# The output projection as seven products of half blocks instead of eight

## Chip, cores and metric

The kernel runs on one core of one Trainium2 chip. The metric is the device time of one execution in microseconds (us); a run list gives its median over several runs. The engines are named as in the profile: PE (matmul, with its weight loader PEld), DVE (vector), ACT (scalar), POOL (general purpose), and SP, which issues most transfers. Each engine executes its own instructions strictly in the order of the program; an instruction that waits holds up all that stand behind it on that engine.

## Reference

One layer of a hybrid attention backbone: 1024 tokens, 1024 channels, two attention branches, a gated merge, an output projection, a residual with LayerNorm, and a SwiGLU feed-forward with a convolution. The part that the change touches:

```python
def _merge_branches(o_a, o_b, gate_logits, w_branch_a, w_branch_b, w_out):
    g_a, g_b = jnp.split(jax.nn.sigmoid(gate_logits), 2, axis=-1)
    return (g_a * (o_a @ w_branch_a) + g_b * (o_b @ w_branch_b)) @ w_out
...
        h = x * (1.0 + scale1) + shift1
        y = _latent_token_mixer(h, kv_ctx, w_in[l], b_in[l], attn_sink[l], q_norm_g[l], k_norm_g[l],
                                w_branch_a[l], w_branch_b[l], w_out[l], rope)
        x = _layer_norm(DEEPNORM_ALPHA * x + gate1 * y, ln1_g[l], ln1_b[l])

        h = x * (1.0 + scale2) + shift2
        y = _conv_ffn(h, w_up[l], conv_w[l], conv_b[l], w_down[l])
```

## The kernel before

Data lies transposed: channels on the 128 partitions (8 feature tiles f of 128 channels, KT = 8), tokens along the free dimension (T = 1024, two halves of HALF = 512). Every float32 matrix product is done as three matmuls with split operands (`mm3`, lines 90 to 92): each operand is a rounded high part and the low part that is left, and the products high x high, low x high and high x low are added up in PSUM. So each weight and each activation must first be split: a cast for the high part (`split`, line 82 on ACT) and a subtraction for the low part (line 87, on DVE or POOL as the caller says).

The order of stages on PE is: modulation and projections, gates (`gate`, from the weights `wg`, about 100 to 310 us), attention with the branch products A, attention B, the branch products B (tiles `b1_f`, 720 to 763.8 us here), the output projection (tiles `y`, 763.8 to about 857), then the up projection (tiles `u`), the convolution, and the down projection. PE's order in the projection is written out by hand (`manual_schedule`); a scheduler places the other engines' instructions around it, and they then run in that order.

Branch B and the merge. For f = 2 to 7, `b1_f` is multiplied by its gate on DVE (line 1111), and `merge` adds branch A (line 1089) and splits the sum m into `mh` (ACT) and `ml` (DVE).

Output projection. `wout_start` loads one block of `w_out` (128 x 1024, through a raw buffer `rwo`), splits it (`hwo` on ACT, `lwo` on DVE), loads the residual tiles `z` from x and scales them on POOL (line 1083). `y_pair(f, s)` computes the output tiles f and f + 1 for the tokens s: 2 x 8 x 3 matmuls into one PSUM tile of the pool `big` (3 buffers). Then `wout_z` adds gate1 times the result to `z` (line 1222, DVE), and `ln_add` adds up the sum `zs` (POOL for the first half of the tokens, DVE for the second) and the sum of squares `zq` (a square on ACT, an addition on DVE) over the eight tiles. The first half of the tokens is done for all f, then the second half; its last four tiles are done in two slices of 256 tokens (LN1_S is 512, 256 and 256 tokens), so that LayerNorm can begin with a part.

LayerNorm. `ln_steps` makes a list of steps: small matmuls `sta` that add up `zs` and `zq` over the channels (lines 1179, 1180), the variance (DVE, one POOL power, line 1193), a broadcast of mean and scale by PE (line 1201), and for each f an `apply` (lines 1209 to 1213) and `emit1`, which makes the next stage's inputs `B` and the next residual `zo`. `tick` is called between matmuls and releases the next step when enough matmul columns have gone by; LN1_F is the wait before the first step and LN1_D the waits after it, for each of the three slices. A larger number puts a step later in PE's order.

Tiles in SBUF come from a list of slots: `ht` takes one and `hput` gives one back, so that a new tile waits for the last reader of the slot that it gets.

Of the kernel before, what the change touches and what calls it, by code (L numbers as in the profile page):

```python
# [7 lines left out]
F32 = mybir.dt.float32  # L8
# [29 lines left out]
LN1_F = 3500.0, 2000.0, 2000.0  # L38
LN1_D = (2500.0, 2000.0, 2500.0), (2500.0, 1000.0, 700.0), (2500.0, 1000.0, 700.0)
# [30 lines left out]
def layer_kernel(  # L70
# [53 lines left out]
    zd = [dpool.tile([P, T], F32, tag=f"zd{f}", name=f"zd{f}") for f in range(KT)]  # L124
    sgd = [dpool.tile([P, T], F32, tag=f"sg{f}", name=f"sgd{f}") for f in range(2 * KT)]
# [640 lines left out]

    sgp = [None]

    def gate(f, hf):
# [303 lines left out]
    wts = {}  # L1073

    def wout_start(f, rtag="raw"):
        wts[f] = weight(w_out[f], f"wo{f}", 8, tag=None if f < 4 else "wd" if f & 2 else "w", he=nc.scalar,
                        le=nc.vector, rtag=rtag)
        for hf in (0, 1):
            if f < 4:
                zt_[f, hf] = ht(f"z{f}_{hf}", (P, 2, HALF))  # L1080
            z = zv(f, hsl(hf))
            nc.sync.dma_start(z, xT[f][:, hsl(hf)])
            nc.gpsimd.tensor_scalar(out=z, in0=z, scalar1=ALPHA, scalar2=0.0, op0=ALU.mult, op1=ALU.add)

    def merge(f, parts=(slice(0, T),)):
        m = bT[0, f]
        mh, ml = ht(f"mh{f}", dt=R32), ht(f"ml{f}", dt=R32)
        for s in parts:
            nc.vector.tensor_tensor(out=m[:, s], in0=m[:, s], in1=bT[1, f][:, s], op=ALU.add)
            split(m[:, s], mh[:, s], ml[:, s], nc.scalar, nc.vector)  # L1090
        hput(f"bT0_{f}", f"bT1_{f}")
        mrg.append((mh, ml))
# [4 lines left out]
    for f in range(2, KT):  # L1097
# [14 lines left out]
        merge(f, [slice(hs[0] * HALF, (hs[-1] + 1) * HALF) for hs in halves])  # L1112
# [3 lines left out]
        if f in (5, 7):  # L1116
            wout_start(f // 2 - 2, None)
# [103 lines left out]
    def wout_z(f, s, ps, first):  # L1221
        nc.vector.scalar_tensor_tensor(out=zv(f, s), in0=ps, scalar=modc[:, 16 + f:17 + f], in1=zv(f, s),
                                       op0=ALU.mult, op1=ALU.add)
        ln_add(zv(f, s), zs, zq, s, first, f"a{f}_{s.start}", nc.vector,
               nc.vector if s.start else nc.gpsimd)
# [12 lines left out]
    def emit1(f, s):  # L1238
# [8 lines left out]
        if hf:  # L1247
            if f < 4 and c.start == 0:
                tp["v", f] = ht(f"v{f}", (P, 2, HALF))
            v = tp["v", f % 4][:, f // 4, c]  # L1250
            o = z
        else:
            o = ht(f"zo{f}", (P, w))
            hput(f"zo{f}")
            if f % 2:
                nc.gpsimd.tensor_scalar(out=o, in0=z, scalar1=lnx[:, 16 + f:17 + f], scalar2=lnx[:, 24 + f:25 + f],
                                        op0=ALU.mult, op1=ALU.add)
            else:
                residual(o, f, z)
# [60 lines left out]
    def y_pair(f, s, first=False):  # L1320
        w = s.stop - s.start
        ps = big(f"y{f}_{s.start}_{w}")
        for a in (0, 1):
            mm_ticked(ps[:, a * HALF:a * HALF + w], wts[f + a], mrg, s)
        for a in (0, 1):
            wout_z(f + a, s, ps[:, a * HALF:a * HALF + w], first and a == 0)
# [610 lines left out]
```

## Time and profile before

| what | value |
|---|---|
| median of 3 runs | 1523.68 us (1523.13 to 1526.4) |
| profiled execution | 1523.1 us, its span 1521.3 us |
| PE busy | 1503.2 us (99%) |
| DVE, ACT, POOL busy | 1168.3, 786.1 and 751.3 us |
| chain that ended last | PE 92% |
| output projection, tiles `y` | 763.8 to about 857 us |
| its matmuls | 288 of 512 columns, 192 of 256 |

The profile is one execution. The span is from its first to its last instruction, and 1.8 us lie around it. In a row of groups the columns are line, engine, operation, tiles with their shapes, count, busy time and mean duration (ns), and after the second bar the idle time of that engine just before, with what ended it. In a row of the timeline the first number is the start, the second the duration of the group; in brackets stands the idle time before it and the instruction that ended it. In a row of waits stand the total, how often, and the longest. In a row of one tile or line come shortest, median and longest duration in ns, then the first and the last start. A window's row has busy time and count of PE, PEld, DVE, ACT and POOL, the granted clock of PE, the share of time in which DMA engines were busy, and GB/s.

### The profile page before, as it was taken

What the parts mean: (1) busy time and instruction counts of PE and PEld (TensorE: products, weight loads), DVE (VectorE), ACT (ScalarE), POOL (GpSimd) and SP (SyncE); (2) the same over time, 40 slices, a digit from 0 to 9 for tenths busy, and PEclk for the clock granted to TensorE, in tenths of its full rate; (3) what the DMA queues carried; (4) which work ended last, traced back from release to release, by engine and by line L of the source; (5) the groups of instructions that cost most, each with busy time, mean ns of one, the idle gap of its engine ahead of it and who ended that gap; (6) DMA issues with size and microseconds to landing.
All of it is one profiled execution on the core that took longest, in us unless ns stands there. A gap on an engine that the chain in (4) does not pass through costs nothing.

```text
span 1521.3 us, 22183 instructions
## 1 busy us (share of the span) xinstructions
PE 1503.2 (99%) x7812; PEld 1263.3 (83%) x7812; DVE 1168.3 (77%) x1751; ACT 786.1 (52%) x1303; POOL 751.3 (49%) x727
## 2 busy tenths in 40 slices
PE   8999999999999999999999999999999999999997
PEld 7888888888988888887888998888888888888887
DVE  6667986539988787877865788888888888557884
ACT  5322222439988677667234555444444444435552
POOL 0356532426776677766124346666666773111121
PEclk9999999999999999999999999999999999999998
DMA  9777672322234576653541322333344448996731
GB/s 370 266 242 242 223 252 87 106 82 68 67 108 104 131 172 167 153 121 89 207 160 42 104 77 98 111 111 111 111 111 111 112 111 238 340 271 210 255 105 56
DMA packets 114399, 232.09 MB, mean 153 GB/s; under 512 B 13200, under 2 KB 28048, under 8 KB 114192
## 3 DMA queue, kind: packets, MB, share of 16 engines
q1 hardware_dynamic: 99056, 201.82, 39.8%
q0 software_dynamic: 10400, 20.19, 8.8%
q10 hardware_dynamic: 4832, 8.68, 1.5%
q8 instruction: 61, 1.00, 0.3%
q14 instruction: 50, 0.41, 0.1%
HBM read 179.45 MB, written 65.86 MB: 161 GB/s over the span
## 4 chain that ended last, share of the span: by engine, by line
PE 92%; DVE 3%; ACT 2%; issue 1%; DMA 1%; POOL 1%; SPq 0%; DVEq 0%; ACTq 0%; POOLq 0%
PE ptr L604 5%; PE p L90 4%; PE p L91 4%; PE p L92 4%; PE g L90 4%; PE g L92 4%; PE g L91 4%; PE av L627 4%; PE av L628 3%; PE b L90 3%; PE b L92 3%; PE b L91 3%; PE s L496 3%; PE s L497 3%; PE c L90 2%; PE c L92 2%
## 5 line engine op out<-in xcount | busy, mean ns | idle before, releaser
L616 DVE TENSOR_TENSOR ptl<-ptr,pth 128x512 fp32r<-128x512 f32 x195 | 128.2, 685 | 20.2 <-ACT pth L615 18.0
L547 ACT ACTIVATE p<-p,nm 128x1280 f32<-128x1280 f32 (+2 forms) x128 | 139.8, 1093 | 6.6 <-DVE p L545 5.9
L87 DVE TENSOR_TENSOR ld<-rd,hd 128x1024 fp32r<-128x1024 f32 x77 | 94.8, 1250 | 50.5 <-ACT hd L82 48.3
L615 ACT CAST pth<-ptr 128x512 fp32r<-128x512 f32 x195 | 111.3, 590 | 30.3 <-PE ptr L604 28.7
L82 ACT CAST hd<-rd 128x1024 fp32r<-128x1024 f32 x77 | 79.3, 1048 | 82.2 <-PE p L92 55.7
L604 PEld LDWEIGHTS ptr<-identr,pb 128*128 128x128 f32 x944 | 96.3, 140 | 23.7 <-ACT pb L550 3.0
L604 PE MATMUL ptr<-identr,pb 128*128 128x128 f32 x944 | 107.5, 245 | 1.5 <-ACT pb L550 1.0
L87 POOL TENSOR_TENSOR wlg<-wg,whg 128x512 fp32r<-128x512 f32 x32 | 48.6, 1529 | 121.7 <-ACT whg L82 80.8
L627 PE MATMUL av<-pth,VT 128*128 128x512 f32 x236 | 104.2, 441 | 0.5 <-ACT side L639 0.3
L90 PE MATMUL p<-hd 128*128 128x512 f32 x264 | 103.2, 391 | 0.0
L92 PE MATMUL p<-hd,ld 128*128 128x512 f32 x264 | 102.8, 389 | 0.0
L91 PE MATMUL p<-ld,hd 128*128 128x512 f32 x264 | 102.7, 389 | 0.0
L90 PE MATMUL g<-hh,whg 128*128 128x512 f32 x256 | 99.9, 390 | 0.0
L92 PE MATMUL g<-hh,wlg 128*128 128x512 f32 x256 | 99.7, 389 | 0.0
L91 PE MATMUL g<-hl,whg 128*128 128x512 f32 x256 | 99.6, 389 | 0.0
L628 PE MATMUL av<-ptl,VT 128*128 128x512 f32 x236 | 97.5, 413 | 0.3 <-DVE ptl L616 0.2
L545 DVE TENSOR_SCALAR_CACHE_REDUCE p<-s,cvt,nmc 128x1024 f32<-128x1024 f32 x64 | 84.2, 1317 | 5.2 <-PE s L497 5.2
L496 PE MATMUL s<-KL,q 128*128 128x512 f32 (+2 forms) x192 | 73.6, 384 | 1.3 <-DVE p L545 0.8
L497 PE MATMUL s<-KL,q 128*128 128x512 f32 (+2 forms) x192 | 71.8, 374 | 0.0
L783 ACT ACTIVATE sg<-g,bgc 128x512 f32<-128x512 f32 x32 | 22.0, 686 | 96.2 <-PE g L92 91.4
L82 ACT CAST wS<-s 128x512 fp32r<-128x512 f32 x76 | 45.3, 620 | 48.7 <-POOL s L1236 47.9
L82 ACT CAST wA<-ru 128x512 fp32r<-128x512 f32 x57 | 35.5, 623 | 62.6 <-PE d L92 33.6
(434 smaller groups left out, 4866.9 us busy)
## 6 DMA issues: line engine op xcount, KB each, us to landing
wml<-in_wmodT_dram SPq DMA_DIRECT2D x48, 512.0 KB
ru<-in_w_up_dram SPq DMA_DIRECT2D x38, 512.0 KB
rd<-td SPq DMA_DIRECT2D x55, 256.0 KB
rd<-sd SPq DMA_DIRECT2D x44, 256.0 KB
rd<-in_w_dn_dram SPq DMA_DIRECT2D x33, 256.0 KB
wm<-in_wmodT_dram SPq DMA_DIRECT2D x16, 512.0 KB
wg<-in_w_g_dram SPq DMA_DIRECT2D x32, 256.0 KB
sgd<-sg ACTq DMA_DIRECT2D x32, 256.0 KB
```

The lines of the kernel that those rows point to most:

```text
L82: nc.scalar.copy(hi, src)
L87: lo_eng.tensor_tensor(out=lo, in0=src, in1=hi.bitcast(F32), op=ALU.subtract)
L90: nc.tensor.matmul(ps, a[0], b[0], start=start, stop=False, skip_group_check=resumed)
L91: nc.tensor.matmul(ps, a[0], b[1], start=False, stop=False, skip_group_check=resumed)
L92: nc.tensor.matmul(ps, a[1], b[0], start=False, stop=stop, skip_group_check=resumed)
L496: nc.tensor.matmul(o, self.q[0][:, hs], ks, start=True, stop=False)
L497: nc.tensor.matmul(o, self.q[1][:, hs], ks, start=False, stop=stop)
L547: nc.scalar.activation(row, row, AF.Exp, bias=self.nm[:, hs], scale=-1.0, accum_out=self.sm[:, hs])
L604: i = nc.tensor.transpose(tr[:, h * P:(h + 1) * P], self.bits[:, h, n * P:(n + 1) * P], identr)
L616: nc.vector.tensor_tensor(out=lo, in0=tr, in1=hi.bitcast(F32), op=ALU.subtract)
L627: nc.tensor.matmul(self.av, v, hi, start=first, stop=False)
L628: nc.tensor.matmul(self.av, v, lo, start=False, stop=self.left == 0)
```

## The change

The 8 x 8 blocks of `w_out` and the 8 x 2 blocks of the merged activations m are taken as 2 x 2 half blocks: weights by output tiles (f below 4, from 4) and by input tiles k (below 4, from 4), activations by k and by token half. Instead of the eight products of half blocks, seven are made, numbered 1, 2, 6, 7, 4, 5, 3 in this order (`WSEQ`). Each has two groups g = 0, 1 of two output tiles (`wprod`, 2 x 4 x 3 matmuls of 512 columns); product 3 is made in two slices of 256 tokens. Products 2, 4 and 3 are added in PSUM onto the tiles of products 1, 7 and 5 (`WFROM`); before that, the engines that need product 1, 7 or 5 alone have read it.

The sums on the weight side (four tiles `wod` in DRAM) are made during the gates, by copies on SP's queue (`wo_put`) and accumulating transfers on POOL's queue (`wo_acc`). The sums on the activation side (`mbuild`) are made in place during the branch products B on DVE and POOL, and then split (`W4` to `W7`). The output tiles are put together from the products on ACT (copies `wx`, then scaled copies `wy` and `wx`), on DVE (`gacc`, from PSUM) and on POOL (`gsum`, from the copies). The 14 weight groups (each 128 x 1024) are split on ACT and POOL (before: 8 of this size on ACT and DVE). The scaling of `z` goes from POOL to ACT, and the residual `zo` is made on ACT alone (before: every second on POOL). LN1_F and LN1_D of the first slice are smaller.

```diff
-LN1_F = 3500.0, 2000.0, 2000.0
-LN1_D = (2500.0, 2000.0, 2500.0), (2500.0, 1000.0, 700.0), (2500.0, 1000.0, 700.0)
+LN1_F = 2000.0, 2000.0, 2000.0
+LN1_D = (1500.0, 1500.0, 1500.0), (2500.0, 1000.0, 700.0), (2500.0, 1000.0, 700.0)
...
+    def wo_block(f, c):
+        return w_out[f:f + 4][:, :, 4 * c:4 * c + 4].rearrange("n p k q -> p n (k q)")
+    def wo_put(n, src):
+        nc.sync.dma_start(wod[n], src)
+    def wo_acc(n, src):
+        nc.gpsimd.dma_start(wod[n], src, accum_op=ALU.add)
+    wo_sums = {4: lambda: (wo_put(1, wo_block(4, 0)), wo_put(3, wo_block(0, 0))),
+               7: lambda: (wo_acc(1, wo_block(4, 1)), wo_acc(3, wo_block(4, 0))),
+               9: lambda: wo_put(2, wod[1]), 11: lambda: wo_acc(2, wo_block(0, 0)),
+               12: lambda: wo_put(4, wod[2]), 14: lambda: wo_acc(4, wo_block(0, 1))}
...
+    def z_start(f, hf):
+        z = zt_[f, hf] = ht(f"z{f}_{hf}", (P, 2, HALF))
+        for a in (0, 1):
+            nc.sync.dma_start(z[:, a], xT[f + 4 * a][:, hsl(hf)])
+        nc.scalar.mul(z, z, ALPHA)
...
+        for hf in parts:
+            if f >= 4 or hf == 0:
+                t = mB[f, hf] = ht(f"m{f}_{hf}", (P, 2, HALF), R32)
+                if hf:
+                    nc.scalar.mul(t[:, 0], m[:, hsl(1)], -1.0)
+                    nc.vector.scalar_tensor_tensor(out=t[:, 1], in0=m[:, hsl(1)], scalar=-1.0,
+                                                   in1=t[:, 0].bitcast(F32), op0=ALU.mult, op1=ALU.subtract)
+                else:
+                    split(m[:, hsl(0)], t[:, 0], t[:, 1], nc.scalar, nc.vector)
...
+    def mbuild(k):
+        sub(nc.vector, b11, b12, b11)
+        sub(nc.gpsimd, b12, b22, b12)
+        sub(nc.vector, b22, b22, b11)
+        parts(6, b22, nc.vector)
+        sub(nc.gpsimd, b21, b22, b21)
+        parts(7, b12, nc.vector)
+        parts(4, b21, nc.gpsimd if k % 2 else nc.vector)
+        parts(5, b11, nc.gpsimd)
...
+    WSEQ = 1, 2, 6, 7, 4, 5, 3
+    WSRC = {1: (0, 0), 2: (0, 1), 4: (4, 1), 5: 1, 6: 2, 7: 3, 3: 4}
+    def wout_load(p, first=False):
...
+                r = post.tile([P, 2, HALF], F32, tag="raw", name=f"rwo{p}_{g}", bufs=3)
...
+            nc.sync.dma_start(r, src)
...
+            split(r, h, l, nc.scalar, nc.gpsimd)
...
+    WFROM = {2: 1, 4: 7, 3: 5}
+    for g in (0, 1):
+        for a, o in enumerate(wprod(1, g)):
+            nc.scalar.copy(wx[2 * g + a], o)
...
+        for a, o in enumerate(wprod(2, g)):
+            gacc(2 * g + a, h0, o)
+            zadd(2 * g + a, h0, g + a == 0)
...
+        for a, o in enumerate(wprod(6, g)):
+            f = 2 * g + a
+            sub(nc.vector, wx[f], o, wx[f])
+            nc.scalar.activation(wy[f], wx[f], AF.Identity, scale=modc[:, 20 + f:21 + f])
+            nc.scalar.activation(wx[f], wx[f], AF.Identity, scale=ngain[:, f:f + 1])
+            gsum(f + 4, h0, wy[f])
+            gsum(f + 4, h1, wy[f])
+            gsum(f, h1, wx[f])
...
+        for a, o in enumerate(wprod(7, g)):
+            gacc(2 * g + a + 4, h1, o, True)
...
+        for a, o in enumerate(wprod(4, g)):
+            f = 2 * g + a + 4
+            gacc(f, h0, o, True)
+            zadd(f, h0)
     pend += ln1(0)
...
+        for a, o in enumerate(wprod(5, g)):
+            f = 2 * g + a + 4
+            gacc(f, h1, o)
+            zadd(f, h1, f == 4)
+    for g in (0, 1):
         for si in (1, 2):
+            for a, o in enumerate(wprod(3, g, slice(s.start - HALF, s.stop - HALF))):
+                gacc(2 * g + a, s, o, True)
+                zadd(2 * g + a, s)
```

What this does to the order of the engines is shown at three places. A number at the end of a tile's name is that of its buffer; the number before it tells the feature tile, the product and its group, or the half.

ACT at the end of the branch products B, where the merged sums of feature tile 7 are cast (`mh7` before; `m7`, `W5_3`, `W7_3` after) and the weights `hwo` are cast. Before:

```order
L82 CAST mh6_8729<-bT0_6_6525 128x1024
L82 CAST mh7_8764<-bT0_7_6743 128x512 x2
L82 CAST hwo2_8799<-rwo2_8797 128x1024
L82 CAST hwo3_8811<-rwo3_8809 128x1024
L82 CAST hwo4_8879<-rwo4_8877 128x1024
```

After, for the same place:

```order
L82 CAST m7_0_8813<-bT0_7_6755 128x512
L82 CAST hwo2_0_8869<-rwo2_0_8867 128x1024
L82 CAST W5_3_8847<-bT0_3_5963 128x512
L82 CAST hwo2_1_8875<-rwo2_1_8873 128x1024
L1106 ACTIVATE m7_1_8831<-bT0_7_6755 128x512
L82 CAST W7_3_8841<-bT0_3_5963 128x512
L1424 COPY wx0_8865<-y1_0_8879 128x512 x2
```

The copies of product 1 (`wx0`) now stand on ACT behind the casts of sums that need feature tile 7, and `W7_3` behind a subtraction on POOL.

POOL ahead of the first LayerNorm statistics, where it adds the last `zs` and then computes the power `rsa0`. Before:

```order
L1147 TENSOR_TENSOR zs1_8793<-zs1_8793,z1_0_8778 128x512
L1147 TENSOR_TENSOR zs1_8793<-zs1_8793,z2_0_8803 128x512
L1147 TENSOR_TENSOR zs1_8793<-zs1_8793,z3_0_8815 128x512
L1193 TENSOR_TENSOR rsa0_9134<-rsa0_9134,mhalf_72 128x4
L1143 TENSOR_SCALAR zs1_8793<-z0_1_8698 128x512
```

After:

```order
L1388 TENSOR_TENSOR z3_1_9052<-z3_1_9052,wx1_8866 128x512
L87 TENSOR_TENSOR lwo3_0_9279<-rwo3_0_9276,hwo3_0_9278 128x1024
L87 TENSOR_TENSOR lwo5_0_9199<-rwo5_0_9196,hwo5_0_9198 128x1024
L87 TENSOR_TENSOR lwo3_1_9285<-rwo3_1_9282,hwo3_1_9284 128x1024
L87 TENSOR_TENSOR lwo5_1_9205<-rwo5_1_9202,hwo5_1_9204 128x1024
L1218 TENSOR_TENSOR zs1_8859<-zs1_8859,z0_0_8933 128x512
L1218 TENSOR_TENSOR zs1_8859<-zs1_8859,z1_0_8937 128x512
L1218 TENSOR_TENSOR zs1_8859<-zs1_8859,z2_0_8941 128x512
L1218 TENSOR_TENSOR zs1_8859<-zs1_8859,z3_0_8945 128x512
L1264 TENSOR_TENSOR rsa0_9334<-rsa0_9334,mhalf_72 128x4
```

The low parts of the weights of products 3 and 5, and the `gsum` additions before them, now stand in front of the last four `zs` additions.

DVE between the application of LayerNorm to the first half and the two slices of the last product, where the results leave PSUM (`y5_0` holds products 5 and 3 after the change; line 1381 is `gacc`). Before:

```order
L1236 TENSOR_TENSOR B7_0_9383<-z3_0_8815,B7_0_9383 128x512
L1222 SCALAR_TENSOR_TENSOR z0_1_8698<-y4_512_256_9285,modc_60,z0_1_8698 128x256
L1222 SCALAR_TENSOR_TENSOR z1_1_8781<-y4_512_256_9285,modc_60,z1_1_8781 128x256
L1147 TENSOR_TENSOR zs1_8793<-zs1_8793,z0_1_8698 128x256
L1148 TENSOR_TENSOR zq1_8794<-zq1_8794,sqa4_512_9354 128x256
```

After:

```order
L1282 TENSOR_TENSOR z2_0_8941<-z2_0_8941,bcma0_9360 128x512
L1280 TENSOR_TENSOR z2_0_8941<-z2_0_8941,bcra0_9355 128x512
L1381 SCALAR_TENSOR_TENSOR z0_1_9040<-y5_0_9300,ngain_8861,z0_1_9040 128x256
L1219 TENSOR_TENSOR zq1_8860<-zq1_8860,sqa6_512_9417 128x512
L1218 TENSOR_TENSOR zs1_8859<-zs1_8859,z0_1_9040 128x256
L1302 TENSOR_TENSOR B1_0_9408<-z1_0_8937,B1_0_9408 128x512
L1219 TENSOR_TENSOR zq1_8860<-zq1_8860,sqa7_512_9422 128x512
L1381 SCALAR_TENSOR_TENSOR z1_1_9044<-y5_0_9300,ngain_8861,z1_1_9044 128x256
```

Before, both slices had PSUM tiles of their own (`y4_512_256`, `y4_768_256`) and the first half's LayerNorm was over on DVE when the first slice was taken; after, one PSUM tile holds both slices, and the taking of the first stands among that LayerNorm's steps.

More of the change, by code (lines that the diff above doesn't have):

```diff
@@ L1085, in merge @@
-    def merge(f, parts=(slice(0, T),)):
-        m = bT[0, f]
[L1087 to L1092, printed above, removed]
+    mB, mT = {}, {}
+    wor = {}
+    def z_start(f, hf):
[3 more added lines that the diff above has]
+        nc.scalar.mul(z, z, ALPHA)
@@ new lines, in merge @@
+    def merge(f, parts=(0, 1)):
+        m = bT[0, f]
+        s = slice(parts[0] * HALF, (parts[-1] + 1) * HALF)
+        nc.vector.tensor_tensor(out=m[:, s], in0=m[:, s], in1=bT[1, f][:, s], op=ALU.add)
+        for hf in parts:
[7 more added lines that the diff above has]
+                    split(m[:, hsl(0)], t[:, 0], t[:, 1], nc.scalar, nc.vector)
+        if parts[-1]:
+            hput(f"bT1_{f}")
@@ L1111, in layer_kernel @@
             nc.vector.tensor_tensor(out=b, in0=ps, in1=b, op=ALU.mult)
-        merge(f, [slice(hs[0] * HALF, (hs[-1] + 1) * HALF) for hs in halves])
+            if len(hs) == 1:
+                merge(f, hs)
+        if len(halves) == 1:
+            merge(f)
+        if f >= 4:
+            mbuild(f - 4)
         if f == 3:
@@ L1254, in emit1 @@
             hput(f"zo{f}")
[L1255 to L1259, printed above, removed]
+            residual(o, f, z)
         nc.sync.dma_start(zd[f][:, s], o)
@@ L1318, in up_weights, with gacc, zadd, gsum @@
         upw[j, gv] = wring(w_up[2 * j + gv], f"wu{gv}_{j}", le=nc.vector, which=which)
[L1320 to L1326 removed]
+    ngain = tiny("ngain")
+    nc.vector.tensor_scalar(out=ngain, in0=modc[:, 16:24], scalar1=-1.0, scalar2=None, op0=ALU.mult)
+    def gacc(f, s, src, neg=False):
+        nc.vector.scalar_tensor_tensor(out=zv(f, s), in0=src, scalar=ngain[:, f:f + 1] if neg else modc[:, 16 + f:17 + f],
+                                       in1=zv(f, s), op0=ALU.mult, op1=ALU.add)
+    def zadd(f, s, first=False):
+        ln_add(zv(f, s), zs, zq, s, first, f"a{f}_{s.start}", nc.vector, nc.vector if s.start and f < 4 else nc.gpsimd)
+    def gsum(f, s, src):
+        nc.gpsimd.tensor_tensor(out=zv(f, s), in0=zv(f, s), in1=src, op=ALU.add)
+    WOP = {1: lambda k: mB[k, 0], 2: lambda k: mB[k + 4, 0], 3: lambda k: mB[k + 4, 1]}
+    WFROM = {2: 1, 4: 7, 3: 5}
+    wps = {}
+    def wprod(p, g, c=slice(0, HALF)):
+        h, l = wor[p, g]
+        w = c.stop - c.start
+        more = p in WFROM
+        if more:
+            ps = wps[WFROM[p], g]
+        else:
+            ps = wps[p, g] = big(f"y{p}_{g}")
+        for a in (0, 1):
+            o = ps[:, a * HALF + c.start:a * HALF + c.stop]
+            for k in range(4):
+                b = WOP[p](k) if p < 4 else mT[p, k]
+                n = slice(k * P, (k + 1) * P)
+                mm3(o, (h[:, a, n], l[:, a, n]), (b[:, 0, c], b[:, 1, c]), not more and k == 0, k == 3, more)
+                tick(w / 0.8)
+        return [ps[:, a * HALF + c.start:a * HALF + c.stop] for a in (0, 1)]
     def ln1(si):
@@ new lines, in layer_kernel @@
+    wout_load(7)
+    wy = four("y")
+    for f in range(4):
+        z_start(f, 1)
+    for g in (0, 1):
+        for a, o in enumerate(wprod(6, g)):
[6 more added lines that the diff above has]
+            gsum(f, h1, wx[f])
```

95 lines of the change are left out of this document (57 added, 38 removed).

## Prediction

> **What bounds the kernel now.** I read the page's first and fourth parts, then the waits of the matrix engine around the output projection, then its timeline there, and last the groups of the engines that feed it.
>
> ```profile
> span 1521.3 us, 22183 instructions
> PE 1503.2 (99%) x7812; PEld 1263.3 (83%) x7812; DVE 1168.3 (77%) x1751; ACT 786.1 (52%) x1303; POOL 751.3 (49%) x727
> PE 92%; DVE 3%; ACT 2%; issue 1%; DMA 1%; POOL 1%; SPq 0%; DVEq 0%; ACTq 0%; POOLq 0%
> PE sta L1180 <- DVE zq L1148: 0.4, 2, 0.2
> L90 PE MATMUL y<-mh,hwo x160: 277/389/476, 763.8 to 856.3; 128*128 128x512 f32 x96, 128*128 128x256 f32 x64
> 760.00:780.00 20.00, 20.00 (x90) 16.57 (x89) 14.88 (x18) 8.89 (x10) 6.57 (x8) 1.00 0.78 253
> 780.00:800.00 20.00, 20.00 (x90) 16.57 (x89) 10.11 (x11) 3.19 (x6) 5.32 (x4) 1.00 0.18 61
> 820.00:840.00 20.00, 20.00 (x120) 17.82 (x119) 16.06 (x24) 16.21 (x25) 16.40 (x13) 1.00 0.25 93
> ```
>
> PE (tensor engine) makes the time: it is busy 99%, and in the projection (763.8 to about 856.6) the only wait put down to it is 0.4 us before the LayerNorm sums. The windows give busy us of PE, its weight loader, DVE (vector), ACT (scalar) and POOL, then the granted clock (full) and the DMA share: the helpers are half idle until 820. So fewer matmuls pay in full only while the helpers deliver in time; the change takes work from PE and hands it to them.
>
> **The saving.**
>
> ```profile
> 827.82 0.39 PE L91 MATMUL y<-ml,hwo 128*128 128x512 f32 x1
> 832.12 0.39 PE L92 MATMUL y<-mh,lwo 128*128 128x512 f32 x1
> 832.35 0.28 PE L90 MATMUL y<-mh,hwo 128*128 128x256 f32 x1
> 833.78 0.28 PE L90 MATMUL y<-mh,hwo 128*128 128x256 f32 x1
> ```
>
> From the first to the second row are 19 matmuls, 4.30/19 = 0.226 us each; from the third to the fourth 12, 1.43/12 = 0.119 us each. Before: 288 x 0.226 + 192 x 0.119 = 88.0 us; the other 4.8 of the 92.8 are LayerNorm matmuls. After: seven products of 48 matmuls, six in 512 columns (288 x 0.226) and the seventh twice in 256 (96 x 0.119). **Saved: 96 x 0.119 = 11.4 us** (10.9 if counted as 48 wide ones). A product's group (24 matmuls) takes 5.44 us. Without waits the groups would end at 763.8 + 5.44 n: product 1 at 769.2 and 774.7, 2 at 780.1 and 785.6, 6 at 791.0 and 796.4, 7 at 801.9 and 807.3, 4 at 812.8 and 818.2; the first LayerNorm matmul (sta) stands 12 matmuls into product 5, at 820.9.
>
> **What the helpers get: three places where PE can stop.**
>
> ```profile
> L87 POOL TENSOR_TENSOR O<-ot,O x31: 729/741/750, 353.0 to 715.2; 128x256 fp32r<-128x256 f32 x31
> L87 POOL TENSOR_TENSOR ptl<-side,pth x41: 1284/1297/1308, 356.6 to 706.4; 128x512 fp32r<-128x512 f32 x41
> L1147 POOL TENSOR_TENSOR zs<-zs,z 128x512 f32<-128x512 f32 x7 | 10.0, 1435 | 22.9 <-DVE z L1222 22.6
> L87 DVE TENSOR_TENSOR ml<-bT,mh 128x512 fp32r<-128x512 f32 x2 | 1.4, 686 | 0.7 <-ACT mh L82 0.7
> L1089 DVE TENSOR_TENSOR bT<-bT,bT 128x1024 f32<-128x1024 f32 x7 | 9.1, 1298 | 0.2
> L1111 DVE TENSOR_TENSOR bT<-b,bT 128x1024 f32<-128x1024 f32 x5 | 6.1, 1221 | 0.9 <-PE b L92 0.9
> L1222 DVE SCALAR_TENSOR_TENSOR z<-y,modc,z 128x512 f32<-128x512 f32 x12 | 8.5, 746 | 16.0 <-PE y L92 16.0
> L82 ACT CAST mh<-bT 128x512 fp32r<-128x512 f32 x2 | 1.2, 620 | 3.6 <-DVE bT L1089 3.6
> L82 ACT CAST hwo<-rwo 128x1024 fp32r<-128x1024 f32 x8 | 8.4, 1049 | 8.4 <-DMA rwo<-in_w_out_dram 7.1 <-DVE ml L87 1.3
> ```
>
> POOL adds or subtracts two 128x512 tiles in 1.29 us alone, 1.435 beside DVE. No row has it at 128x1024; 0.55 more per 256 columns (0.741 to 1.297) makes 2.4 us, and twice the 512 price 2.6 to 2.9. I take 2.4 at the low end, 2.67 (scaled by 1.435/1.29) as my value.
>
> *A, product 2.* It accumulates on product 1's PSUM, so it waits for ACT's copies wx, due at 774.7. They stand on ACT behind casts of the sums for tile 7, which need the merge of feature tile 7. DVE reaches that from the end of b4 (three tiles of 5.44 before 763.8, so 747.5) through six 128x1024 adds (3 x 1.298 + 3 x 1.221), fourteen 512 ones at 0.686 and three negated parts at 0.746: 19.4 us, 766.9; three waits for ACT's cast (0.62 each) make it 768.8. Then two ACT casts (0.62, 1.05), three POOL steps (2.4, 1.29, 1.29), a cast and two copies (3 x 0.62): 8.5 us, 777.3. **2.6 us late; I take 3**; 0.7 without the cast waits, 6 if DVE and POOL slow each other by a seventh.
>
> *C, the LayerNorm sums.* sta needs the last four zs additions. From product 6's first end (791.0) POOL has, in one queue: two low parts of weights for product 4, twelve additions of scaled tiles (gsum), four low parts for products 3 and 5, the four zs. The first low part can begin after its cast, 792.0. At the low price 6 x 2.4 + 16 x 1.29 = 35.0, ending 827.0, 6 us after 820.9. At 1.435 and 2.67 it is 39.0, ending 831.0: **10 us late, my value.** Before, POOL finished zs just in time, and had nothing between:
>
> ```profile
> 808.40 3.00 POOL L1147 TENSOR_TENSOR zs<-zs,z 128x512 f32<-128x512 f32 x2 [7.88 <-DVE z L1222]
> 812.00 0.38 PE L1180 MATMUL sta<-onec,zq 128*128 128x1 f32 x2 [0.17 <-DVE zq L1148]
> 764.70 1.33 SPq L1021 DMA_DIRECT2D rwo<-in_w_out_dram  x3
> 768.88 1.05 ACT L82 CAST hwo<-rwo 128x1024 fp32r<-128x1024 f32 x1 [1.69 <-DMA rwo<-in_w_out_dram]
> ```
>
> The upper end is 17.5: 1.5 and 2.9 per step (41.4) and 5 us later start, since a weight load now waits on the in-order SP queue for one of three raw buffers that POOL's low parts free; a load is used about 4 us after its issue (764.70 to 768.88), and the residual loads (z) stand in the same queue. Product 4's second group also needs the twelfth gsum and two DVE steps: at 814.6 + 1.5 against 812.8 it is part of C's lateness, not added.
>
> *D, product 3 in two slices.* Both write one PSUM tile, so slice two waits until DVE has taken slice one. On DVE stand the LayerNorm applications of the first half ahead of that.
>
> ```profile
> 815.84 0.17 DVE L1188 TENSOR_SCALAR mva<-sta 128x8 f32<-128x8 f32 x1 [3.89 <-PE sta L1180]
> 819.15 1.28 DVE L1209 TENSOR_TENSOR z<-z,bcra 128x512 f32<-128x512 f32 x2 [1.38 <-PE bcra L1201]
> L1209 DVE TENSOR_TENSOR z<-z,bcra 128x512 f32<-128x512 f32 x8 | 5.2, 683 | 1.4 <-PE bcra L1201 1.4
> L1222 DVE SCALAR_TENSOR_TENSOR z<-y,modc,z 128x256 f32<-128x256 f32 x8 | 3.5, 477 | 2.1 <-PE y L92 2.1
> L1147 DVE TENSOR_TENSOR zs<-zs,z 128x256 f32<-128x256 f32 x8 | 3.3, 417 | 0.0
> L1236 DVE TENSOR_TENSOR B<-z,B 128x512 fp32r<-128x512 f32 x4 | 3.9, 976 | 2.4 <-ACT z L1230 2.4
> L87 DVE TENSOR_TENSOR lwu<-rwu,hwu 128x1024 fp32r<-128x1024 f32 x3 | 3.7, 1222 | 0.1
> ```
>
> Count from sta's start: the first application comes 7.15 later (812.00 to 819.15), then ten 0.683 and two 0.746: 15.5; slice one's two parts are taken at 16.0 and, after four more, 18.9. PE has 36 matmuls (8.15) and about 2 of LayerNorm work, then 24 narrow ones (2.9): it wants slice two at 13.1. The part at 18.9 is wanted 1.4 after it: 4.4 late. The second group meets the same after 7.9 us of DVE (nine narrow steps, four of 0.69, one of 1.22): 3.6 late. **8 us**; 4 if the scheduler's gaps fall better, 14 if DVE's additions take 0.976 beside POOL.
>
> *At no cost.* Four copies and four accumulating transfers of 1 MB in the gates: POOL's issue is 1.17 us each, and PE's cover is the gate matmuls.
>
> ```profile
> L1004 POOL DMA_DIRECT2D sd<-in_w_dn_dram x12: 1145/1174/1373, 483.0 to 694.3; - x12
> 140.00:180.00 40.00, 40.00 (x179) 33.10 (x178) 34.67 (x63) 9.97 (x16) 25.57 (x26) 1.00 0.75 247
> L1083 POOL TENSOR_SCALAR z<-z 128x512 f32<-128x512 f32 x16 | 11.8, 751 | 45.6 <-DMA z<-in_xT_dram 44.2 <-DVE ml L87 1.2
> 840.00:857.00 17.00, 17.00 (x144) 16.95 (x143) 12.53 (x28) 6.57 (x12) 2.28 (x2) 1.00 0.24 81
> 840.77 1.36 DVE L1236 TENSOR_TENSOR B<-z,B 128x512 fp32r<-128x512 f32 x1 [0.34 <-ACT z L1230]
> ```
>
> The DMA engines are busy 0.75 there and PE without a gap, so I put 0, up to 5 if a gate's weights come late. The 16 scalings (11.8 us) move from POOL to ACT, busy 3 to 9 of 20 us until 800: 0. What leaves DVE (the weights' low parts) is already out of the lists in A and D. The earlier numbers for the first half's LayerNorm put sta 6 matmuls (1.4 us) sooner; after it u's first matmul is only about 25 us off instead of 45 (812 to 857), against 30 for its last input on DVE (812.0 to 842.1), but the inputs are read one after another and D's 8 us lie between: 0, up to 4 if D vanishes.
>
> The Trainium skill's page "SBUF — State Buffer", section "Who interferes with whom", says that a DVE instruction with two SBUF inputs and a POOL instruction that reads SBUF exclude each other for their whole length.
>
> ```profile
> 786.71 2.99 POOL L1147 TENSOR_TENSOR zs<-zs,z 128x512 f32<-128x512 f32 x2 [6.89 <-DVE z L1222]
> 787.26 2.99 DVE L1148 TENSOR_TENSOR zq<-zq,sqa 128x512 f32<-128x512 f32 x2
> ```
>
> Here two POOL additions and two DVE additions run together, each 1.5 us instead of 1.29 and 0.69: slowed, yet less than the 1.98 per pair that taking turns would make. The Trainium skill's rule would put C higher by at most DVE's seven 512 and two 1024 steps there, 7.3 us, and the time at 1540.
>
> **Sum.** -11.4 + 3 + 10 + 8 = +9.6 on the profiled execution (span 1521.3 and 1.8 around it, 1523.1; the median of the runs is 0.6 higher, 1523.7): **1533 us**. All low: 0.7 + 6 + 4 = 10.7, 1522.4. All high: 37.5, 1549.2.
>
> **Rivals.** *POOL keeps up* (faster): if a 128x1024 low part costs about 1.4 us, hardly more than a 512 one, C falls by 6 x 1.27 = 7.6 to 2.4 and A by 1.3 to 1.7; with D at its 4 the waits are 8 and the time 1519.7. It decides where the waits stay under 8.4 (11.4 less the 3 us, 0.2%, that a measurement of this kernel tells from nothing). Against it: 256 to 512 columns nearly doubles POOL's time. With all waits gone it would be 1511.7. *They cancel*: low ends in all three, 1522. *Worse*: a late gate weight (5) or taking turns (7.3) beside my sum, 1538 to 1549, or all high.
>
> **Chances.** The forecast, waits of 14.4 to 32 (1526 to 1544): 0.55; worse, above 1544: 0.12; cancelled, 1520.6 to 1526.7: 0.11; faster: 0.22, of it 0.1 below 1515. Slower in all 0.67. The range leaves out about 0.1 at each end: 1515 to 1549; the forecast's own is 1526 to 1544.
>
> **What would show it.** PE with 96 fewer matmuls; PE waits at product 2 for ACT's wx, at sta for POOL's zs, and at product 3 for DVE's z, of about 3, 10 and 8 us; POOL nearly without idle time from 792 to sta. Wrong if POOL idles there while PE doesn't wait, if 128x1024 on POOL is far from 2.4 to 2.9, or if PE waits in the gates or at u.

## The result, and the profile after

The changed kernel takes 1573.45 us (median of 4 runs, 1570.07 to 1581.85), the kernel before 1524.1 us on the same chip: a ratio of 1.033 (95% interval 1.0285 to 1.0374). The forecast was 1533, range 1515 to 1549. The direction was right, the size was not: 49 us above the kernel before instead of 9.

The page of the profiled execution (1571.2 us), its span, busy times and chain:

```profile
span 1569.4 us, 22114 instructions
PE 1514.1 (96%) x7716; PEld 1264.0 (81%) x7716; DVE 1186.0 (76%) x1770; ACT 816.9 (52%) x1352; POOL 816.5 (52%) x754
PE 83%; DVE 4%; DMA 3%; ACT 3%; issue 3%; POOL 2%; SPq 0%; DVEq 0%; ACTq 0%; POOLq 0%
```

PE has 96 fewer instructions (7716 instead of 7812) and is busy 11 us longer, since a matmul at a lower clock counts as busy for longer. Its waits, in total, number and longest:

```profile
PE y L90 <- DVE z L1381: 12.8, 3, 5.8
PE sta L1250 <- POOL zs L1218: 11.4, 1, 11.4
PE y L90 <- ACT wx L1424: 9.5, 1, 9.5
PE accka L91 <- DVE wlka L87: 4.0, 2, 2.1
PE sta L1251 <- DVE zq L1219: 0.8, 1, 0.8
```

Before, PE's only wait that the profile puts down in the projection was the one at sta, 0.4 us in two parts. Windows of 20 us, with the busy time of PE first and the granted clock and the DMA share near the end of a row:

```profile
200.00:220.00 20.00, 20.00 (x90) 16.57 (x89) 17.66 (x27) 4.98 (x9) 10.18 (x7) 1.00 1.05 350
220.00:240.00 20.00, 17.86 (x72) 14.27 (x71) 7.71 (x15) 2.45 (x4) 1.16 (x1) 0.91 0.94 287
780.00:800.00 20.00, 10.54 (x38) 8.17 (x37) 12.89 (x15) 11.56 (x17) 15.71 (x9) 0.74 0.32 111
840.00:860.00 20.00, 7.83 (x32) 6.14 (x32) 12.13 (x8) 6.40 (x8) 13.60 (x7) 0.76 0.49 157
```

Two things stand there beside idle time: the clock falls to 0.74 and 0.76 in windows that hold waits, and the DMA engines are full at 200 to 220 us (share 1.05). The timeline of PE at product 2 shows the clock at work:

```profile
791.96 0.80 PE L90 MATMUL y<-m,hwo 128*128 128x512 f32 x1 [9.46 <-ACT wx L1424]
792.55 0.63 PE L91 MATMUL y<-m,hwo 128*128 128x512 f32 x1
795.96 0.63 PE L90 MATMUL y<-m,hwo 128*128 128x512 f32 x1
796.90 0.40 PE L90 MATMUL y<-m,hwo 128*128 128x512 f32 x1
```

After the wait the matmuls come 0.427 us apart (792.55 to 795.96: eight steps in 3.41 us) instead of 0.226, and return to the old pace after 4 to 5 us. The Trainium skill's page "TensorE: Matmul & The Clock Gate", Part 1, says that the clock halves after an idle window of about 3.4 us and comes back after a busy one; these rows agree, for a wait of 9.46 us.

From the first matmuls of each stage, the 48.1 us between the two spans lie as follows:

| stretch | before | after | difference |
|---|---|---|---|
| start to the first `y` | 763.8 | 771.5 | +7.7 |
| first `y` to first `u` | 92.9 | 128.4 | +35.5 |
| first `u` to first `p` (down projection) | 430.7 | 432.0 | +1.3 |
| first to last `p` | 181.7 | 185.0 | +3.3 |
| last `p` to the end | 52.2 | 52.5 | +0.3 |

The 35.5 are 11.4 saved, 34.5 of waits (9.46 for wx, 4.07 in product 4, 11.41 and 0.76 at sta, 5.84 and 2.91 in product 3), and about 12.5 of matmuls at the lower clock behind them. This is PE's account only; whether each item is a cost of its own is what the experiments are for.

### The profile page after: what moved, and what is told of

Its sections match the earlier page's. It is cut to its first block, busy times and chain, and to the rows that moved or that the text cites. A ratio compares the mean times of both kernels' runs of the same rounds, so it can differ in the third digit from the quotient of the medians.

```text
span 1569.4 us, 22114 instructions
## 1 busy us (share of the span) xinstructions
PE 1514.1 (96%) x7716; PEld 1264.0 (81%) x7716; DVE 1186.0 (76%) x1770; ACT 816.9 (52%) x1352; POOL 816.5 (52%) x754
## 4 chain that ended last, share of the span: by engine, by line
PE 83%; DVE 4%; DMA 3%; ACT 3%; issue 3%; POOL 2%; SPq 0%; DVEq 0%; ACTq 0%; POOLq 0%
PE ptr L605 4%; PE p L90 4%; PE p L91 4%; PE p L92 4%; PE av L628 4%; PE av L629 3%; PE g L90 3%; PE g L91 3%; PE g L92 3%; PE s L497 3%; PE s L498 3%; PE b L90 2%; PE b L91 2%; PE a L91 2%; PE d L91 2%
## 5 line engine op out<-in xcount | busy, mean ns | idle before, releaser
L87 POOL TENSOR_TENSOR wlg<-wg,whg 128x512 fp32r<-128x512 f32 x32 | 43.7, 1375 | 108.1 <-ACT whg L82 108.1
```

The source lines that it names most:

```text
L87: lo_eng.tensor_tensor(out=lo, in0=src, in1=hi.bitcast(F32), op=ALU.subtract)
```

## Experiments

Each was timed beside the kernel before on one chip: e1 to e4 against 1524.41 us, e5 to e8 against 1524.81, e9 to e12 against 1524.6. "Stage" is the time from the first `y` to the first `u`; it was 128.4 in the changed kernel. The 95% interval of the changed kernel's ratio (1.0285 to 1.0374) is some 14 us wide and holds the ratios of e2, e4, e5, e6, e7 and e9; so for these runs, and for e10 just below it, the time by itself shows little, and the trace has to show where it went.

| run | median, us | ratio to before | first `y` | stage |
|---|---|---|---|---|
| e1: before, with the sums of weights | 1533.46 | 1.0058 (1.0043 to 1.0073) | 774.7 | 93.0 |
| e2: matmuls to fill the sta wait | 1573.67 | 1.032 (1.0304 to 1.0335) | 773.3 | 128.6 |
| e3: low parts on DVE | 1563.2 | 1.0253 (1.0233 to 1.0274) | 773.8 | 118.6 |
| e4: sums moved in the program | 1575.82 | 1.034 (1.0324 to 1.0355) | 776.2 | 128.4 |
| e5: sums held back | 1567.96 | 1.0286 (1.0269 to 1.0303) | 766.4 | 129.6 |
| e6: wx ahead of the last splits | 1569.78 | 1.0297 (1.0278 to 1.0316) | 770.4 | 126.0 |
| e7: product 3 by slices | 1570.63 | 1.0304 (1.0289 to 1.032) | 773.6 | 124.0 |
| e8: e3, e5, e6, e7 together | 1551.09 | 1.0181 (1.0156 to 1.0205) | 770.4 | 109.1 |
| e9: matmuls to fill all long waits | 1579.39 | 1.036 (1.0346 to 1.0374) | 770.4 | 136.9 |
| e10: ngain made later | 1567.41 | 1.0282 (1.0268 to 1.0296) | 772.4 | 128.2 |
| e11: before, buffers 192 bytes higher | 1529.53 | 1.0036 (1.0024 to 1.0048) | 764.0 | 92.6 |
| e12: e8, e10 and fills | 1546.99 | 1.0145 (1.0131 to 1.0159) | 764.9 | 112.6 |

### The early transfers: e1, e4, e5

e1 is the kernel before with the eight transfers added in the gates; nothing reads their results.

```diff
+        if hf and f in wo_sums:
+            wo_sums[f]()
```

> The kernel before with only the weight sums of the change added (the copies and the accumulating transfers in the gates); nothing reads their results. Theory T (the transfers fill the DMA engines while the key and value weights wka are loaded): PE waits about 4 us for the low parts of wka between 219 and 254 us, the projection starts at 771 instead of 764, and the time is 6 to 9 us above the kernel before. Rival R (the late start after the change has another cause, such as a new order or placement of the instructions): the projection starts at 764 and the time is within 2 us of before.

The wait of PE in e1, then the window of 200 to 220 us in the kernel before and in e1:

```profile
PE accka L91 <- DVE wlka L87: 7.3, 2, 4.3
```

```profile
200.00:220.00 20.00, 20.00 (x90) 16.57 (x89) 19.61 (x27) 5.33 (x10) 8.95 (x6) 1.00 0.69 240
```

```profile
200.00:220.00 20.00, 20.00 (x90) 16.53 (x90) 15.82 (x27) 4.85 (x9) 9.17 (x7) 1.00 1.05 349
```

The transfers alone cost 9 us, with waits of 7.3 us for these weights where 4 were expected. The DMA share goes from 0.69 to 1.05 at 200 to 220 us, and the next stage's weights arrive late. In the changed kernel the wait on DVE is the end of a chain that begins with a transfer, as the longest wait of the casts of these weights on ACT shows (idle time in brackets):

```profile
232.47 0.62 ACT L82 CAST whka<-wka 128x512 fp32r<-128x512 f32 x1 [8.01 <-DMA wka<-in_w_kv_dram]
```

In the changed kernel the 7.7 us of later start are, by PE's timeline, 4.0 of these waits, 3.4 of matmuls 0.427 us apart behind them, and 0.3 of other things. Here the lower clock was a cost, since nothing made it up before the first `y`.

e4 called the sums from the attention's units 1 to 11 instead of from the gates:

```diff
-        if hf and f in wo_sums:
-            wo_sums[f]()
...
+        if u in wo_sums:
+            wo_sums[u]()
```

> The changed kernel with the copies and accumulating transfers of the weight sums moved from the gates into the first eleven units of attention, where the DMA engines are busy about a quarter of the time. Theory T (they cost only because they meet the key and value weights): no wait for wka, the projection starts at 764 to 765, the time falls by 6 to 9 us, and the waits inside the projection stay at 34 us. Rival P (POOL's issue of the four accumulating transfers, 1.2 us each, or their traffic costs as much in attention): new waits of PE between 340 and 480 us, and a fall of under 2 us.

The expectation missed: nothing in the program holds these transfers back, and the scheduler placed them earlier (the first at 76.8 us; in the changed kernel at 127.1). The new wait of PE, and the window that holds it:

```profile
PE accqa L90 <- ACT whqa L82: 7.9, 1, 7.9
```

```profile
100.00:120.00 20.00, 12.13 (x43) 9.27 (x42) 8.15 (x12) 2.90 (x5) 11.61 (x10) 0.74 1.06 270
```

The same congestion, 100 us earlier. e5 made the order a dependence: each sum's tile in DRAM reuses the place of a tile whose reader runs late, in attention's units 19 to 29; the trace has the transfers at 457 to 648 us.

```diff
+        wod[n] = dpool.tile([P, 4, HALF], F32, tag=tokens.pop(), name=f"wo{n}")
```

> The changed kernel with the weight sums held back: their tiles in DRAM take the places of tiles whose last reader is late, so that the first copies can only start in the second half of attention (units 19 to 29 of 32). In the run before this one a mere move in the program did not hold them: the scheduler issued them earlier than in the changed kernel, and PE waited 7.9 us for the weights wqa instead of 4 us for wka. Theory T (they cost wherever they meet loads that PE is about to need): no wait of PE for wka or wqa, the gates end as before the change, the projection starts at 764 to 767, and the time falls by 5 to 9 us. Rival P (the traffic costs as much there): new waits of PE of 4 us or more between 480 and 720, and a fall of under 2 us.

```profile
220.00:240.00 20.00, 20.00 (x90) 16.57 (x89) 9.59 (x18) 5.05 (x10) 1.28 (x1) 1.00 0.57 187
```

PE is full again there, and the first `y` comes at 766.4 instead of 771.5; the run is 5.5 us faster. So theory T holds. What is left of the 7.7 us is 2.6, of which a new wait in attention for POOL takes 2.0.

### The queues in the projection: e3, e6, e7

e3 puts the low parts of the weights of products 7, 4, 5 and 3 on DVE.

```diff
-            split(r, h, l, nc.scalar, nc.gpsimd)
+            split(r, h, l, nc.scalar, nc.vector if p in (7, 4, 5, 3) else nc.gpsimd)
```

> The changed kernel with the low parts of the weights of products 7, 4, 5 and 3 made on DVE instead of POOL. Theory C (POOL's queue sets the wait before LayerNorm): the wait of 11.4 us for zs falls below 4, the one of 4 us in product 4 below 2, and the time falls by 9 to 14 us. Rival D (DVE is as full): the waits for DVE before the slices and at product 2 grow, and the time stays within 4 us of the changed kernel.

The waits of PE, and DVE's group of low parts from 800 to 860 us:

```profile
PE sta L1250 <- POOL zs L1218: 4.1, 1, 4.1
```

```profile
L87 DVE TENSOR_TENSOR lwo<-rwo,hwo 128x1024 fp32r<-128x1024 f32 x8 | 12.0, 1524 | 4.0 <-ACT hwo L82 3.9
```

The wait at sta falls from 11.4 to 4.1 us (below 4 was expected), the one in product 4 from 4.1 to 2.3 (below 2 was expected), and the time by 10. On POOL these steps take longer (a group of the changed kernel, 790 to 860 us):

```profile
L87 POOL TENSOR_TENSOR lwo<-rwo,hwo 128x1024 fp32r<-128x1024 f32 x11 | 27.2, 2486 | 8.5 <-ACT hwo L82 8.5
```

So POOL's queue does hold sta up, by 7.3 us of the 11.4 at least. The last column adds what the forecast had not: 8.5 us in which POOL waits for ACT's casts of the same weights.

e6 makes the splits of the last activation sums for products 7 and 4 after the copies wx; the subtractions ahead of them stay where they were, and the low part for product 4 goes from POOL to DVE.

```diff
+            if k == 3:
+                parts(5, b11, nc.gpsimd)
+                return
...
+    mbuild(3, True)
```

> The changed kernel with the last activation sums for feature tile 7 that products 7 and 4 need (W7_3, W4_3) split only after product 1, so that on ACT the copies wx no longer stand behind the cast that waits for POOL. Theory A (the wait of 9.5 us at product 2 is made by ACT's order): that wait falls to 4 us or less at its first group, possibly 2 to 3 more at its second, the first matmuls after it are not slow any more, and the time falls by 4 to 8 us. Rival Q (POOL's low part of product 2's weights or DVE's backlog ends as late): the wait stays above 7 us, or the later waits for POOL grow by what this one loses, and the time stays within 2 us.

```profile
PE sta L1255 <- POOL zs L1223: 12.4, 1, 12.4
PE y L90 <- ACT wx L1429: 6.2, 2, 5.8
```

The wait for wx loses 3.3 us, and sta gains 1.0 of it; 5.8 are left at the first group, where 4 or less were expected. So ACT's order made a part of the wait. On ACT the copies now stand behind the cast of tile 7's merge (783.05) and the casts of product 2's weights (1.99 us), and the rest of the wait is put down to these; this is read from the trace, and no run tried it.

e7 runs both groups of product 3 in the first slice, then both in the second.

```diff
-    for g in (0, 1):
-        for si in (1, 2):
+    for si in (1, 2):
+        for g in (0, 1):
```

> The changed kernel with the four parts of product 3 in another order: the first slice of both groups, then the second slice of both, so that PE has 2.9 us more before it needs a PSUM tile back. Theory D (the two waits of 5.8 and 2.9 us there come from the tile that both slices share): they fall to 5 us together or less, and the time by 3 to 6 us. Rival L (LayerNorm of the first half on DVE is the limit whatever the order): DVE's work comes due later instead, the waits at the second slices and at the LayerNorm matmuls of the slices together stay at 8 us or more, and the time stays within 2 us.

```profile
PE y L90 <- DVE z L1381: 7.3, 3, 4.0
PE sta L1251 <- DVE zq L1219: 3.4, 2, 2.6
```

The waits for DVE's `z` fall from 12.8 to 7.3 us in all. Of the 7.3, 4.7 belong to product 4; the two of 5.8 and 2.9 at the second slices are one of 2.6 now, as theory D had it. A new one of 2.6 appears, for the squares of the next LayerNorm slice, which now has less work ahead of it, so that the stage is 4.4 us shorter; the time falls by 2.8 only, because in this run the stage also begins 2.1 later (5.6 us of waits in the gates).

e8 joins e3, e5, e6 and e7.

> The changed kernel with four edits together: sums held back, copies first, slices swapped, and the low parts of products 7, 4, 5 and 3 on DVE (alone this one gave 10 us). If the causes are separate and add up, the fall is 10 + 7 + 5 + 4 = 26 us, a time of 1545 to 1550, still 20 us above the kernel before, with about 15 us of waits left in the projection. If they share a limit (DVE), the fall is under 18 us.

```profile
PE y L90 <- ACT wx L1430: 7.8, 2, 5.8
PE sta L1257 <- DVE zq L1225: 3.4, 2, 2.6
PE sta L1256 <- POOL zs L1224: 3.1, 1, 3.1
PE y L90 <- DVE z L1387: 2.6, 1, 2.6
```

The stage takes 109.1 us instead of 128.4. These 19.3 us are more than the 16.6 that e3, e6 and e7 gave there one by one (9.8, 2.4 and 4.4), so the three causes in the projection add up. The first `y` comes 4.0 us later than in e5, though, after a wait for POOL in attention of 3.3 us (2.0 in all in e5) and matmuls at the lower clock behind it; the time falls by 22, between the 26 and the 18 of the two expectations. These waits (16.9 us) and the slow matmuls behind them are still more than the 11.4 us that the change saves.

### The lower clock: e2, e9

Are the slow matmuls a cost of their own? e2 put 40 matmuls that nobody reads ahead of the first sta:

```diff
+                if nm == "a0":
+                    warm(40)
```

> The changed kernel with 40 extra matmuls of 512 columns, whose result is not used, put in front of the first LayerNorm matmul, where PE waited 11.4 us; at 0.227 us each they fill 9.1 us of that wait. Theory K (a wait also costs by the slower clock after it, and this adds up with the waits): the matmuls after the LayerNorm sums are 0.227 us apart instead of 0.43, and the time falls by 5 to 7 us. Rival H (behind that wait the next one, for DVE before the second slice, is the limit): the matmuls are faster in the same way, but the wait before the second slice grows by as much from 5.8 us, and the time stays within 2 us of the changed kernel.

```profile
859.36 0.38 PE L1253 MATMUL sta<-onec,zs 128*128 128x1 f32 x2 [1.84 <-POOL zs L1219]
860.70 0.58 PE L1254 MATMUL sta<-onec,zq 128*128 128x1 f32 x2 [0.96 <-DVE zq L1220]
861.15 0.77 PE L90 MATMUL y<-W,hwo 128*128 128x512 f32 x1
```

It decided nothing: waits of 1.84 and 0.96 us were left, the clock fell all the same, and so neither theory was tried. e9 filled all five long waits (40, 17, 48 and 4, 25, 12 matmuls).

> The changed kernel with extra matmuls of 128 x 512 (0.227 us each, results not used) just ahead of the five long waits of PE in the projection: 40 before product 2, 17 before the second group of product 4, 48 before the first zs statistic and 4 behind it, 25 and 12 before the second slices of product 3. They fill the waits and nothing else changes. Theory K (an idle PE loses its granted clock, and the 12.5 us of slow matmuls behind the waits are a cost of their own): no window of the projection shows a granted clock below 0.9, no matmuls 0.427 us apart, and the time falls by 8 to 13 to 1560 to 1565. Theory N (the spacing of 0.427 us is something else that goes with these places, such as traffic to SBUF or PSUM, or what is gained is waited for again): rows 0.427 us apart stay, or the time stays within 3 us of 1573.

PE's timeline at product 2, where the 40 fill the wait:

```profile
784.68 5.83 PE L1209 MATMUL dm<-m 128*128 128x512 f32 x25
791.03 0.50 PE L90 MATMUL y<-m,hwo 128*128 128x512 f32 x1 [0.52 <-ACT wx L1436]
791.37 0.40 PE L91 MATMUL y<-m,hwo 128*128 128x512 f32 x1
791.60 0.39 PE L92 MATMUL y<-m,lwo 128*128 128x512 f32 x1
```

The matmuls behind it are 0.34 and then 0.23 us apart, so at this place the idle time is the cause of the low clock. The time did not follow. The waits of PE:

```profile
PE dm L1209 <- DVE z L1294: 6.8, 1, 6.8
PE y L90 <- ACT sqa L1225: 4.1, 1, 4.1
```

The first is of the experiment's own making: in product 3 the filling matmuls waited 6.8 us for their PSUM buffer. Behind it one window still stands at 0.83. The second stands in front of product 7, where there had been no wait, and it goes with another order on ACT: in this run seven of the eight scalings of `z` stand ahead of the first square `sqa`, in the changed kernel and in e2 to e8 four. The first square in the changed kernel and in e9:

```profile
807.87 0.62 ACT L1217 ACTIVATE sqa<-z 128x512 f32<-128x512 f32 x1
```

```profile
813.47 0.62 ACT L1225 ACTIVATE sqa<-z 128x512 f32<-128x512 f32 x1
```

DVE takes the results of product 2's second group behind that square's addition, at 815.95 instead of 809.44 us, and product 7 needs their PSUM buffer; it began at 817.5 instead of 816.05. So theory K holds for the clock at product 2. For the time the run decides nothing: both waits, 10.9 us together, came with the edit. Whether the 12.5 us are a term that can be taken off by itself, while other engines set the pace, stays open.

### Where the buffers lie: e10, e11

In the changed kernel the `p` matmuls, whose code the change does not touch, come 0.2310 us apart instead of 0.2267 (rows in a window of 20 us: 88 instead of 90), at a granted clock of 1.00 and without a wait. In e1 they keep the old pace. The small tile `ngain` is the first to be made in its pool after the change; with its 6 buffers of 32 bytes it moves the weight buffers `raw` and `wd`, and all that use their place later, up by 192 bytes. e10 makes it after them, e11 puts such a tile in front of them in the kernel before.

```diff
-    ngain = tiny("ngain")
...
     wout_load(2)
+    ngain = tiny("ngain")
```

> The changed kernel with only the small tile ngain (and its one DVE operation) made after the first weights of the projection instead of before them. By that the buffers raw and wd and all that lie behind them in SBUF keep the addresses that they have in the kernel before; with ngain made first they lie 192 bytes higher. Theory P (this shift makes the p matmuls of the last product 0.2310 us apart instead of 0.2267): the p rows go back to 0.2267 apart, 182 instead of 185 us from first to last, the waits in the projection stay, and the time falls by 3 to 5 to 1568 to 1570. Rival R (the p pace comes from the other tiles' slots, or from the traffic of the new program): p stays at 185 us, time 1573.

> The kernel before with one small tile of 8 values per partition, and one DVE operation that fills it and that nothing reads, made ahead of the buffers raw and wd, so that these lie 192 bytes higher, as in the changed kernel. Theory P: its p matmuls come 0.2310 us apart, 185 instead of 181.7 us from first to last, and the time rises by 3 to 5 to 1528 to 1530. Rival R: nothing changes, 1524.5.

The `p` matmuls of line 90 in the changed kernel, in e10 and in e11 (shortest, median and longest, first and last start):

```profile
L90 PE MATMUL p<-hd x264: 389/395/481, 1331.9 to 1516.9; 128*128 128x512 f32 x132
```

```profile
L90 PE MATMUL p<-hd x264: 389/389/486, 1330.6 to 1512.3; 128*128 128x512 f32 x132
```

```profile
L90 PE MATMUL p<-hd x264: 389/395/486, 1288.9 to 1473.9; 128*128 128x512 f32 x132
```

Shown from both sides, in the changed kernel and in the one before: 185.0 us with the shift, 181.7 without. Theory P holds in both. Which of the moved buffers does it was not taken apart. From the first `u` to the end of the span the shift costs 4.8 to 5.2 us (669.5 against 664.3 with the change, 669.4 against 664.6 without).

e12 adds e10 and filling matmuls to e8.

> The best version so far (held sums, low parts of products 7, 4, 5, 3 on DVE, split of W7_3 and W4_3 after product 1, slices of product 3 ordered by slice: 1551.1) with ngain made late as well and extra matmuls ahead of its waits (24 and 7 before the groups of product 2, 12 and 4 around the first statistics, 10 before a second slice). Theories K and P together: 8 us of slow matmuls and 4 us of p pace go, 1538 to 1542. If K falls 1546 to 1548; if P falls 1542 to 1546; if both fall 1551.

At 1546.99 it is the fastest version of the change, still 1.0145 times the kernel before. The 1546 to 1548 of its expectation for the case that theory K fails hold it, but its filling matmuls too brought a wait of their own (4.0 us for a PSUM buffer), so this does not settle K. By the medians it gains 4.1 us over e8. The 7.9 us between the two profiled spans are 5.9 won behind `u` (5 of it the price of the place), 5.5 won ahead of `y` (of it 2.3 in a wait of attention for POOL; the rest I can't explain), and 3.5 lost in the stage with the filling matmuls. The kernel before stays the best.

## Why the prediction was wrong, step by step

*The saving* was right: 96 narrow matmuls fewer. Of the prediction's signs of being wrong one came: PE waited in the gates.

*The early transfers* were put at 0, up to 5. They cost 9 alone (e1); in the changed kernel the first `y` came 7.7 later, and holding them back gave 5.1 of it back (e5). The step that failed is "the DMA engines are busy 0.75 there and PE without a gap, so I put 0": 8 MB more in a stretch at 0.7 to 0.75 left no room, and the transfers behind them were the next stage's weights.

*A*, put at 3 and at most 6, was 9.5. The last part of that sum held: from the cast of tile 7's merge to the end of the copies it took 8.9 us (783.0 to 791.9) where 8.5 were worked out. What was too small is mainly DVE's 19.4 us. The merge was due 5.0 us after the first `y`; its first half was done 9.8 after it (781.3), and its cast came 11.5 after it, since on ACT it stood behind a cast that waited 1.1 us for POOL:

```profile
780.64 0.68 DVE L1101 TENSOR_TENSOR bT<-bT,bT 128x512 f32<-128x512 f32 x1
```

```profile
783.04 0.61 ACT L82 CAST m<-bT 128x512 fp32r<-128x512 f32 x1
```

A window of the changed kernel from the end of `b1_4` on shows DVE nearly full (the third of the busy times):

```profile
755.30:783.60 28.30, 27.20 (x121) 22.18 (x119) 25.95 (x28) 10.05 (x18) 13.61 (x9) 1.00 0.25 84
```

Its steps of 512 columns with both inputs in SBUF, priced at 0.686 to 0.746 us, took 0.9 to 2.3 where they began while POOL had an operation running. One such pair:

```profile
777.52 1.78 DVE L1107 SCALAR_TENSOR_TENSOR m<-bT,m 128x512 fp32r<-128x512 f32 x1
```

```profile
776.98 1.76 POOL L1118 TENSOR_TENSOR bT<-bT,bT 128x512 f32<-128x512 f32 x1
```

The Trainium skill's page "SBUF — State Buffer", section "Who interferes with whom", which the prediction weighed and set aside for a pair at 1.5 us each, says that a DVE instruction with two SBUF inputs contends with a POOL instruction that reads SBUF, for a lock that only one of them holds. These rows agree with it: DVE's step ends 0.56 us after POOL's, as if it had begun only then. Six steps of DVE between 754 and 780 us stand so, each ending 0.54 to 0.56 us after POOL's operation; together they took about 5 us more than 0.69 each, which is about the 4.8 us by which the merge was late on DVE. The pair that the prediction set against the rule fits it too: DVE's two additions end at 790.25, 0.55 us after POOL's two at 789.70, and from the first start to the last end the two pairs take 3.54 us, 1.77 a pair and not 1.5. This is read from the traces; no run took POOL's operations away from there.

*C*, put at 10, was 11.4, and e3 confirms POOL's queue as its cause. But the sum that led to 10 was not what happened. It let POOL run without idle time from product 6 on; in fact POOL stood 8.5 us for ACT's casts, and PE came there later itself. That the number came close is luck in part. DVE also began product 2's results late, since the residual tiles came late:

```profile
803.95 1.41 DVE L1381 SCALAR_TENSOR_TENSOR z<-y,modc,z 128x512 f32<-128x512 f32 x2 [8.44 <-ACT z L1096]
```

On SP's queue their transfers stood behind weight loads that waited for a raw buffer:

```profile
787.29 5.53 SPq L1152 DMA_DIRECT2D rwo<-wo  x2
792.91 8.38 SPq L1095 DMA_DIRECT2D z<-in_xT_dram  x8
```

SP's waits for POOL's low parts come to 13.2 us from 771 to 802. Before, the loads of `z` were issued from 740.0 on, ahead of the first `y`. The prediction had this queue in C's upper end only; the 0 for the 16 scalings left out what they wait for. This chain is read from the trace; it was not taken apart by a run. The second group of product 4 was "part of C's lateness, not added"; PE waited 4.1 us there, by itself.

*D*, put at 8 as 4.4 and 3.6, was 8.8 as 5.8 and 2.9: right, and so was the reason, that both slices write one PSUM tile and DVE takes the first among LayerNorm's steps (with another order of the slices 2.6 of the 8.8 were left, e7).

*At u* no wait appeared, as said. LayerNorm's earlier numbers were not tried by themselves.

*Two terms were missing.* The lower clock adds about 12.5 us to PE's account behind the waits of the projection. How much of it is a cost stays open: in e9 and e12 filling the waits gave no time back in the stage, but both runs brought new waits of their own. And 4.9 us come from buffers that lie 192 bytes higher. Of the 38.5 us between the forecast for the profiled execution (1532.7) and its time (1571.2), by PE's account 7.7 are the transfers, 4.9 the place, 6.5 the size of A, 4.1 product 4, about 3 the sizes of C and D, and 12.5 the slow matmuls.

## What to carry to other kernels

A saving of matmuls on a full PE is worth what the engines that feed it can follow: count their queues from what they wait for, transfers and casts among it, not from the first moment at which they could run. A mean DMA share does not tell whether 8 MB find room. In the gates, at about 0.7, they delayed the weights that PE needed next; spread over 457 to 648 us, where the share was 0.64 to 0.69 without them, the new waits for POOL that came with them were 2.0 us in e5, 3.3 in e8 and 1.0 in e12. A move in the program did not keep the transfers out of a stretch here; a dependence did. When matmuls that the change does not touch alter their pace, compare where their operands lie before looking for a wait. A DVE step with two inputs in SBUF beside a POOL operation is priced from the first start to the last end of the pair.

## What the hardware showed that I had not expected

- 192 bytes in the address of the weight buffers, and of the buffers that use their place later, changed the pace of the `p` matmuls with 512 columns from 0.2267 to 0.2310 us, at full clock.
- A wait of 1.9 us can be followed by the lower clock, though the Trainium skill's page "TensorE: Matmul & The Clock Gate", Part 1, speaks of an idle window of about 3.4 us; this measurement does not agree with it. In the gates of the changed kernel eight matmuls came 0.427 us apart, beginning 0.8 us after the wait:

```profile
242.71 0.50 PE L91 MATMUL accka<-wlka,hh 128*128 128x512 f32 x1 [1.86 <-DVE wlka L87]
243.51 0.63 PE L91 MATMUL accka<-wlka,hh 128*128 128x512 f32 x1
243.93 0.63 PE L92 MATMUL accka<-whka,hl 128*128 128x512 f32 x1
```

- A wait of 3.30 us in product 4 of e6 and one of 2.99 us in the gates of e1 were followed by no matmuls at that pace, so the length of the wait alone does not decide it.
- The accumulating transfers of 1 MB landed 14.2 us (median) after their issue, in a stretch where the DMA share reached 1.05.
